# Small parameter loads of a hybrid encoder layer: other queue, other place in the lead-in

## Chip, cores and metric

The kernel runs on one core of a Trainium2 chip. Such a core has a matmul engine (TensorE, PE in the profile; PEld is its loading of weights), VectorE (DVE), ScalarE (ACT), GpSimd (POOL) and SyncE (SP), which here only issues transfers. 16 DMA engines carry the transfers. The metric is the device time in microseconds (us) of one execution, and the median over several runs.

## What is computed

One step of a streaming encoder layer, for 512 prompt rows and 64 sample rows of width 1024 that share the parameters. Cut to what matters here:

```
mod = silu(c) @ w_ada + b_ada                     # 6 vectors of 1024 for each of the two groups
sh1, sc1, gt1, sh2, sc2, gt2 = split(mod, 6)
h = rms_normalize(x) * g_norm_mix * (1 + sc1) + sh1
q, k, v, qi, ki, wi, z, xbc, dt, gate_logits = split(h @ w_in)
...  # sparse attention: an indexer (qi, ki, wi) picks 256 keys for each query
xbc_c = silu(causal_conv(xbc, w_conv, b_conv))    # and a Mamba-2 scan over it
y = rms_normalize(y * silu(z)) * g_ssm_norm
x = x + gt1 * ((g_attn * (o @ w_branch_attn) + g_ssm * (y @ w_branch_ssm)) @ w_out)
h2 = rms_normalize(x) * g_norm_ffn * (1 + sc2) + sh2
x = x + gt2 * ((silu(gate) * up) @ w_down)        # gate, up = split(h2 @ w_gate_up)
```

The conditioning vectors c are two rows of 1024 (4 KB each). b_ada has 6144 numbers (24 KB), g_norm_mix and g_norm_ffn 1024 each (4 KB), g_ssm_norm 2048 (8 KB), b_conv 4096 (16 KB).

## The kernel before

All work is first recorded as a list of operations with their dependences by a planner, the class `Plan`. Its method `order` gives every operation an estimated duration and a place on its engine: at each step it takes the operation that can start first, by due times and priorities. The method `emit` then issues the operations, all by the same line, so every instruction of the trace carries L569, and the names of its tiles tell what it is. `R.after([...])` adds a dependence for the planner alone. On the chip each engine works its list off in order, and waits by semaphores for what an instruction reads, and for a buffer that it writes over to be free.

Products are made of high and low parts: a weight piece `raw` is loaded, ScalarE rounds it to `wh`, VectorE makes the rest `wl`, and three matmuls (`wh` with the high and the low part of h, `hTh` and `hTl`, and `wl` with `hTh`) sum into `mm`. PE's results stand in eight banks: `mm` (two tiles of two banks), and `px` and `py` with two each, which the operations take in turn. A tile `px` that is asked for anew is one of two banks, and the first writer waits for the last reader of what stood there.

The lead-in: SyncE loads the conditioning rows (`rowsS`), the five blocks of x (`xt`, four of 512 KB and one of 256 KB), then blocks of w_ada (`adr`) and w_in (`raw`). GpSimd issues loads by a software queue (q0), SyncE by the common hardware queue (q1). Vectors arrive as rows of 128 and are turned by a PE transpose (a matmul with the unit matrix `ident`), so that each number stands in its own partition: `rowsS` (16 rows, for `cu`, `cth` and `sil`, the silu of c), `rowsD` (48 rows, b_ada, for `badc`) and `rowsA` (64 rows: both norm gains, the scan's gain and the convolution's bias, for `vc`). For each x block ScalarE squares and sums the rows (`xn` written, a scratch result), VectorE scales them to `xn`, and PE transposes x and `xn`. The matmuls `py<-adr,sil` give the shift and scale of the first norm, from which h is made; some later w_ada columns are summed by VectorE (`aacc`).

After the indexer's projections come the scan's step sizes: PE sums decay exponents with a triangular matrix into a `px` bank (`px<-e,tri`, called `pacs` in the code) and into a `py` bank, VectorE negates the first (`nacs`) and adds the second (`wst`). PE then goes on with the projection that gives k and v, `mm<-wh,hTh` with 256 columns, and `py<-kis,qis`, the indexer's scores.

The list `ropes` holds the operations that end the rotary step of the indexer's query heads.

Of the kernel before, what the change touches and what calls it, by code (L numbers as in the profile page):

```python
# [5 lines left out]
F32 = mybir.dt.float32  # L6
# [3 lines left out]
OP = mybir.AluOpType  # L10
# [3 lines left out]
P = 128  # L14
# [562 lines left out]
def build(tc, I, O):  # L577
    R = Plan(tc)
    vec, act, pool, pe, sync = R.vec, R.act, R.pool, R.pe, R.sync
    cp = R.mkpool("const")  # L580
# [5 lines left out]
    sp = R.mkpool("start")  # L586
# [4 lines left out]
    def px(name, tag="px"):  # L591
        return psum.tile([P, 512], F32, name=name, tag=tag, bufs=2)
# [5 lines left out]
    ident = cp.tile([P, P], F32, name="ident")  # L598
# [60 lines left out]
    def pair_order(r):  # L659
        return ORD0 if r == 0 else (1, 7, 6, 2, 5, 4, 3)  # L660
# [162 lines left out]
            pe.transpose(out, ident, ident)  # L823

    rowsS = sp.tile([16, P], F32, name="rowsS")
    for r0, src in ((0, I["c_prompt"][0]), (8, I["c_sample"][0])):
        sync.dma_start(rowsS[r0:r0 + 8], src.rearrange("(a b) -> a b", b=P))
    xt = []
    for tb in range(5):
        n = P if tb < 4 else NS  # L830
        t = sp.tile([P, D], F32, name=f"xt{tb}")
        src = x_p[tb * P:(tb + 1) * P] if tb < 4 else x_s
        sync.dma_start(t[:n], src)
        xt.append(t)


    sil = adp.tile([P, 8, 32], F32, name="sil")
# [7 lines left out]
    pc = px("pc", "py")  # L845
# [90 lines left out]
    def rstd_of(ss, out, n, rows, denom):  # L936
        vec.tensor_scalar(out, ss, 1.0 / denom, EPS, op0=OP.mult, op1=OP.add)
        pow_mhalf(out, out, n)
# [13 lines left out]
    rs = sp.tile([P, 5], F32, name="rs")  # L952
    pool.memset(rs, 1.0)
    turned, xn_ops = [], []
    rowsD = sp.tile([48, P], F32, name="rowsD")
    pool.dma_start(rowsD, I["b_ada"][0].rearrange("(a b) -> a b", b=P))
    rowsA = sp.tile([64, P], F32, name="rowsA")
    for r0, n, src in ((0, 8, I["g_norm_mix"][0]), (8, 8, I["g_norm_ffn"][0]), (16, 16, I["g_ssm_norm"][0]), (32, 32, I["b_conv"][0])):
        pool.dma_start(rowsA[r0:r0 + n], src.rearrange("(a b) -> a b", b=P))
    for tb in range(5):  # L960
        n = P if tb < 4 else NS
        xn = sp.tile([P, D], F32, name=f"xn{tb}", tag="xn", bufs=4)
        act.activation(xn[:n], xt[tb][:n], AF.Square, accum_out=rs[:n, tb:tb + 1])
        rstd_of(rs[:n, tb:tb + 1], rs[:n, tb:tb + 1], 1, n, D)
        xn_ops.append(vec.tensor_scalar(xn[:n], xt[tb][:n], rs[:n, tb:tb + 1], None, op0=OP.mult))
        for k4 in range(2):
            p = px(f"pxn{tb}_{k4}")
            for j in range(4):
                kt = 4 * k4 + j
                turned.append(pe.transpose(p[:, j * P:j * P + n], xn[:n, kt * P:(kt + 1) * P], ident[:n, :n]))  # L970
            act.activation(xnT[:, 4 * k4:4 * k4 + 4, tb * P:tb * P + n], p.rearrange("p (k q) -> p k q", k=4)[:, :, :n], AF.Copy)
        if tb == 2:
            badc = cp.tile([P, 48], F32, name="badc")
            with R.after([turned[-1]]):
                pe.transpose(pc[:, 64:112], rowsD, ident[:48, :48])
            vec.tensor_copy(badc, pc[:, 64:112])
            vc = cp.tile([P, 64], F32, name="vc")
            with R.after([turned[-1]]):
                pe.transpose(pc[:, 128:192], rowsA, ident[:64, :64])
            vec.tensor_copy(vc, pc[:, 128:192])  # L980
            g_mix, g_ffn = vc[:, 0:8], vc[:, 8:16]
    rowsB = sp.tile([P, P], F32, name="rowsB")
    rowsC = sp.tile([96, P], F32, name="rowsC")
    gsh = cp.tile([P, 16], F32, name="gsh")
    vec.tensor_scalar(gsh, vc[:, 16:32], 0.5, None, op0=OP.mult)
    wc = cp.tile([P, 4, 32], F32, name="wc")
    bc_ = cp.tile([P, 32], F32, name="bconv")
    stc = cp.tile([P, 3, 32], F32, name="stc")
    vec.tensor_scalar(bc_, vc[:, 32:64], 0.5, None, op0=OP.mult)

    A1 = cp.tile([P, 8, 2], F32, name="A1")
    hTh = hp.tile([P, 8, T], F32R, name="hTh")
# [30 lines left out]
    with R.prio(-1500):  # L1023
        for tb in range(5):
            n = P if tb < 4 else NS
# [23 lines left out]
    t = px("pwc")  # L1049
# [196 lines left out]
    ropes, masked = [], []  # L1246
# [75 lines left out]
    acs_d = R.dram([32, T], F32, name="acs_d")  # L1322
    sync.dma_start(acs_d, acsT)

    with R.after([ropes[1]]):
        for dst, src in xst:
            sync.dma_start(dst, src)
# [4 lines left out]
    for b in range(5):  # L1332
        n = P * (b + 1) if b < 4 else T
# [3 lines left out]
    for b in (4, 1, 2, 3):  # L1337
        smp = b == 4
        n = T if smp else P * (b + 1)
# [109 lines left out]
    for kv in range(NKV):  # L1449
# [21 lines left out]
        for un in units + [None]:  # L1471
            nxt = None
            if un is not None:
                b, qs, k0, n, nk, v0, w = un
# [316 lines left out]
    for a in range(8):  # L1791
# [5 lines left out]
        with R.prio(MPRIO):  # L1797
            vec.scalar_tensor_tensor(t2(g), t2(g), 1.0, ps, op0=OP.add, op1=OP.mult)
            vec.tensor_tensor(m, m, g, OP.add)
            for c0, n, d0, dn in ((0, NP_, 0, HP), (NP_, NS, HP, HS)):  # L1800
                src = t2(m[:, c0:c0 + n])
# [23 lines left out]
    with R.prio(PTP):  # L1825
        for c0 in PT:
            w = I["w_out"][0]
            b = pair_raw[c0] = {"qs": [PAIRW[p] for p in pair_order(c0 // 256)]}
# [54 lines left out]
    for r in range(NPW):  # L1883
# [3 lines left out]
        t, u, v, zz = ha[:, 0], ha[:, 1], hb[:, 0], hb[:, 1]  # L1887
# [39 lines left out]
    for hf in range(2):  # L1927
# [17 lines left out]
        for j in range(4):  # L1945
            t = y2[j, hf][:, :, 0:TH]
# [185 lines left out]
    for i, (f, w, x, b, starts, *p) in enumerate(steps):  # L2132
# [6 lines left out]
        if i < N0:  # L2139
            if not starts:  # L2140
                with R.prio(4000):
                    n = TH if b[1] == "1" else TW
# [357 lines left out]
```

## Time and profile before

| | |
|---|---|
| median of three runs (lowest, highest) | 1350.63 us (1348.82, 1352.64) |
| the profiled execution | 1350.98 us, of which the span 1349.3 us |
| granted clock of PE over the span | 0.998 of 2.4 GHz |
| moved by DMA | 202.88 MB, mean 150 GB/s |
| software queue (q0) | 5152 packets, 14.87 MB |

The span reaches from the first to the last instruction that the profile shows; the execution's own time is 1.7 us longer. The median is over unprofiled runs. All rows further down come from the one profiled execution.

### The profile page before, as it was taken

How to read it: one execution, taken by the hardware profiler on the slowest of the kernel's cores; microseconds unless marked ns; L12 is line 12 of the kernel's file. 1: busy time of each engine (PE TensorE's matmuls, PEld its weight loads, DVE VectorE, ACT ScalarE, POOL GpSimd, SP SyncE). 2: the span in 40 equal slices, each digit the busy share in tenths (PEclk: the TensorE clock that was granted, in tenths of full speed). 3: DMA queues.
4: the chain of work that ended last, by engine and by line, in shares of the span. 5: the costliest groups of instructions: out<-in, count | busy, mean ns of one | idle time of the engine just before them, and what ended most of it. 6: DMA issues, size and time to landing. Idle time of an engine off the chain costs nothing.

```text
span 1349.3 us, 27924 instructions
## 1 busy us (share of the span) xinstructions
PE 1334.7 (99%) x10601; PEld 1299.7 (96%) x10601; DVE 1162.0 (86%) x2373; ACT 775.9 (58%) x1641; POOL 250.4 (19%) x386
## 2 busy tenths in 40 slices
PE   7999999999999999999999999999999999999998
PEld 6999999999999999999999999999999999999998
DVE  5687999887778798888887798898799999988997
ACT  4564333777776766666565442227576666665553
POOL 2322011330300235545463300000000000000000
PEclk9999999999999999999999999999999999999999
DMA  9874435664854464454445797665433344424352
GB/s 286 249 195 117 112 109 150 153 171 99 196 126 119 132 175 116 115 149 131 131 122 165 231 306 245 208 196 176 117 95 97 99 130 131 124 83 137 100 159 63
DMA packets 269975, 202.88 MB, mean 150 GB/s; under 512 B 26048, under 2 KB 240176, under 8 KB 269840
## 3 DMA queue, kind: packets, MB, share of 16 engines
q1 hardware_dynamic: 264400, 186.09, 47.1%
q0 software_dynamic: 5152, 14.87, 5.7%
q8 instruction: 83, 1.36, 0.4%
q14 instruction: 52, 0.43, 0.1%
q10 hardware_dynamic: 288, 0.13, 0.0%
HBM read 158.33 MB, written 28.96 MB: 139 GB/s over the span
## 4 chain that ended last, share of the span: by engine, by line
PE 91%; DVE 4%; DMA 2%; issue 1%; ACT 1%; SPq 1%; DVEq 0%; ACTq 0%
PE mm L569 63%; PE py L569 16%; PE px L569 12%; DMA adr<-in_w_ada 1%; DMA raw<-in_w_in 1%; DMA xt<-in_x_prompt 1%; DVE aacc L569 1%; DVE wl L569 1%; SPq L569 1%; DVE g L569 0%; ACT wh L569 0%; DVE wh L569 0%; DVE y L569 0%; DVE tok L569 0%; DVE x L569 0%
## 5 line engine op out<-in xcount | busy, mean ns | idle before, releaser
L569 PE MATMUL mm<-hTl,wh 128*128 128x288 f32 (+1 forms) x1088 | 246.9, 302 | 1.1 <-DVE hTl L569 1.1
L569 PE MATMUL mm<-hTh,wh 128*128 128x288 f32 (+1 forms) x1088 | 244.9, 302 | 0.6 <-ACT wh L569 0.5
L569 PE MATMUL mm<-hTh,wl 128*128 128x288 f32 (+1 forms) x1088 | 244.3, 302 | 0.0
L569 ACT ACTIVATE wh<-raw 128x1024 fp32r<-128x1024 f32 (+3 forms) x143 | 137.9, 966 | 124.7 <-PE mm L569 106.7
L569 PEld LDWEIGHTS mm<-hTl,wh 128*128 128x128 f32 (+1 forms) x1088 | 177.1, 189 | 4.0 <-DVE hTl L569 1.8
L569 PEld LDWEIGHTS mm<-hTh,wh 128*128 128x128 f32 (+1 forms) x1088 | 176.0, 189 | 3.9 <-ACT hTh L569 0.8
L569 PEld LDWEIGHTS mm<-hTh,wl 128*128 128x128 f32 (+1 forms) x1088 | 176.1, 189 | 2.2 <-issue 0.7
L569 DVE TENSOR_TENSOR wl<-raw,wh 128x1024 fp32r<-128x1024 f32 (+2 forms) x94 | 117.3, 1250 | 18.2 <-ACT wh L569 16.9
L569 POOL DMA_DIRECT2D wl<-raw x24 | 20.9, 872 | 463.7 <-PE px L569 314.0
L569 PE MATMUL mm<-oh,wh 128*128 128x288 f32 (+1 forms) x424 | 94.8, 299 | 0.3 <-ACT sum L569 0.3
L569 DVE SCALAR_TENSOR_TENSOR cu<-xc,wc,cu 128x579 f32<-128x579 f32 x96 | 83.9, 875 | 2.0 <-ACT cu L569 1.0
L569 PE MATMUL mm<-oh,wl 128*128 128x288 f32 (+1 forms) x360 | 79.9, 298 | 0.0
L569 PE MATMUL mm<-ol,wh 128*128 128x288 f32 (+1 forms) x276 | 72.4, 298 | 0.0
L569 PEld LDWEIGHTS mm<-oh,wh 128*128 128x128 f32 x424 | 70.4, 188 | 1.1 <-ACT sum L569 0.5
L569 DVE SCALAR_TENSOR_TENSOR aacc<-adr,sil,aacc 128x512 f32<-128x512 f32 x84 | 62.8, 785 | 7.0 <-DMA adr<-in_w_ada 7.0
L569 PEld LDWEIGHTS mm<-oh,wl 128*128 128x128 f32 x360 | 59.7, 188 | 0.3 <-issue 0.2
L569 PE MATMUL mm<-yl,wh 128*128 128x288 f32 x256 | 55.0, 295 | 0.0
L569 PE MATMUL mm<-yh,wh 128*128 128x288 f32 x256 | 54.9, 295 | 0.0
L569 PE MATMUL mm<-wl,hTh 128*128 128x256 f32 x192 | 54.6, 285 | 0.3 <-DVE wl L569 0.3
L569 PE MATMUL mm<-wh,hTl 128*128 128x256 f32 x192 | 54.7, 286 | 0.0
L569 PE MATMUL mm<-yh,wl 128*128 128x288 f32 x256 | 54.4, 294 | 0.0
L569 PE MATMUL mm<-wh,hTh 128*128 128x256 f32 x192 | 53.6, 283 | 0.0
(584 smaller groups left out, 3940.9 us busy)
## 6 DMA issues: line engine op xcount, KB each, us to landing
raw<-in_w_in SPq DMA_DIRECT2D x80, 512.0 KB, 4.2
adr<-in_w_ada SPq DMA_DIRECT2D x36, 512.0 KB, 5.4
raw<-in_w_gate_up SPq DMA_DIRECT2D x22, 512.0 KB, 3.9
wl<-raw POOLq DMA_DIRECT2D x21, 512.0 KB, 4.6
rawu<-in_w_gate_up SPq DMA_DIRECT2D x20, 512.0 KB, 4.0
bc<-acs_d SPq DMA_DIRECT2D x32, 256.0 KB, 3.5
raw<-in_w_branch_ssm SPq DMA_DIRECT2D x16, 512.0 KB, 5.0
gate_d<-sg SPq DMA_DIRECT2D x16, 288.0 KB, 2.2
```

The lines of the kernel that those rows point to most:

```text
L569: getattr(engines[x.eng], x.fn)(*[real(a) for a in x.args], **{k: real(v) for k, v in x.kw.items()})
```

## The change

The two conditioning rows are loaded by SyncE behind the second x block rather than ahead of the first. `rowsD` takes g_norm_mix with it: 56 rows, two loads by SyncE behind the x blocks where GpSimd's software queue had loaded them, one transpose and one copy. `rowsA` keeps the other three vectors (56 rows); its three loads are issued by SyncE after the indexer's queries, its transpose goes to a new `px` tile near the scan's step sizes, and `gffn` becomes a tile of its own. GpSimd issues five loads fewer, SyncE five more. The planner makes its order anew from this list.

```diff
     rowsS = sp.tile([16, P], F32, name="rowsS")
-    for r0, src in ((0, I["c_prompt"][0]), (8, I["c_sample"][0])):
-        sync.dma_start(rowsS[r0:r0 + 8], src.rearrange("(a b) -> a b", b=P))
     xt = []
     for tb in range(5):
...
         sync.dma_start(t[:n], src)
         xt.append(t)
+        if tb == 1:
+            for r0, src in ((0, I["c_prompt"][0]), (8, I["c_sample"][0])):
+                sync.dma_start(rowsS[r0:r0 + 8], src.rearrange("(a b) -> a b", b=P))
...
-    rowsD = sp.tile([48, P], F32, name="rowsD")
-    pool.dma_start(rowsD, I["b_ada"][0].rearrange("(a b) -> a b", b=P))
-    rowsA = sp.tile([64, P], F32, name="rowsA")
-    for r0, n, src in ((0, 8, I["g_norm_mix"][0]), (8, 8, I["g_norm_ffn"][0]), (16, 16, I["g_ssm_norm"][0]), (32, 32, I["b_conv"][0])):
-        pool.dma_start(rowsA[r0:r0 + n], src.rearrange("(a b) -> a b", b=P))
+    rowsD = sp.tile([56, P], F32, name="rowsD")
+    for r0, n, src in ((0, 48, I["b_ada"][0]), (48, 8, I["g_norm_mix"][0])):
+        sync.dma_start(rowsD[r0:r0 + n], src.rearrange("(a b) -> a b", b=P))
...
         if tb == 2:
-            badc = cp.tile([P, 48], F32, name="badc")
+            badc = cp.tile([P, 56], F32, name="badc")
             with R.after([turned[-1]]):
-                pe.transpose(pc[:, 64:112], rowsD, ident[:48, :48])
-            vec.tensor_copy(badc, pc[:, 64:112])
-            vc = cp.tile([P, 64], F32, name="vc")
-            with R.after([turned[-1]]):
-                pe.transpose(pc[:, 128:192], rowsA, ident[:64, :64])
-            vec.tensor_copy(vc, pc[:, 128:192])
-            g_mix, g_ffn = vc[:, 0:8], vc[:, 8:16]
+                pe.transpose(pc[:, 64:120], rowsD, ident[:56, :56])
+            vec.tensor_copy(badc, pc[:, 64:120])
+            g_mix = badc[:, 48:56]
     rowsB = sp.tile([P, P], F32, name="rowsB")
     rowsC = sp.tile([96, P], F32, name="rowsC")
+    rowsA = cp.tile([56, P], F32, name="rowsA")
+    g_ffn = cp.tile([P, 8], F32, name="gffn")
     gsh = cp.tile([P, 16], F32, name="gsh")
-    vec.tensor_scalar(gsh, vc[:, 16:32], 0.5, None, op0=OP.mult)
...
-    vec.tensor_scalar(bc_, vc[:, 32:64], 0.5, None, op0=OP.mult)
...
+    with R.after([ropes[3]]):
+        for r0, n, src in ((0, 32, I["b_conv"][0]), (32, 16, I["g_ssm_norm"][0]), (48, 8, I["g_norm_ffn"][0])):
+            sync.dma_start(rowsA[r0:r0 + n], src.rearrange("(a b) -> a b", b=P))
+    t = px("pwd")
+    pe.transpose(t[:, 0:56], rowsA, ident[:56, :56])
+    vec.tensor_scalar(bc_, t[:, 0:32], 0.5, None, op0=OP.mult)
+    vec.tensor_scalar(gsh, t[:, 32:48], 0.5, None, op0=OP.mult)
+    vec.tensor_copy(g_ffn, t[:, 48:56])
```

How the order of the engines changes is shown at two places. The first is the head of SyncE's list, before:

```order
L569 DMA rowsS_140<-in_c_prompt 8x128
L569 DMA rowsS_140<-in_c_sample 8x128
L569 DMA xt_0_141<-in_x_prompt 128x1024
L569 DMA xt_0_142<-in_x_prompt 128x1024
L569 DMA xt_0_143<-in_x_prompt 128x1024
L569 DMA xt_0_144<-in_x_prompt 128x1024
L569 DMA xt_0_145<-in_x_sample 64x1024
L569 DMA adr_158<-in_w_ada 128x4x256
```

and of the change:

```order
L569 DMA xt_0_142<-in_x_prompt 128x1024
L569 DMA xt_0_143<-in_x_prompt 128x1024
L569 DMA rowsS_141<-in_c_prompt 8x128
L569 DMA rowsS_141<-in_c_sample 8x128
L569 DMA xt_0_144<-in_x_prompt 128x1024
L569 DMA xt_0_145<-in_x_prompt 128x1024
L569 DMA xt_0_146<-in_x_sample 64x1024
L569 DMA rowsD_151<-in_b_ada 48x128
L569 DMA rowsD_151<-in_g_norm_mix 8x128
L569 DMA adr_158<-in_w_ada 128x4x256
```

Two x blocks now stand first, and the two `rowsD` loads stand between the x blocks and w_ada. (The number behind a name is the tile's buffer, counted anew in each kernel.)

The second place is PE's list where the projection of k begins, behind the sums with the triangular matrix, before:

```order
L569 MATMUL px_112<-e_0_704,tri_72 128x32
L569 MATMUL py_110<-e_0_704,ones_71 128x32
L569 MATMUL mm_115<-wh_103,hsS_128 128x256
L569 MATMUL mm_115<-wl_106,hsS_128 128x256
L569 MATMUL mm_114<-wh_101,hTh_126 128x256
L569 MATMUL mm_114<-wl_104,hTh_126 128x256
L569 MATMUL mm_114<-wh_101,hTl_127 128x256
L569 MATMUL mm_114<-wh_101,hTh_126 128x256
L569 MATMUL mm_114<-wl_104,hTh_126 128x256
```

and of the change:

```order
L569 MATMUL px_113<-e_0_697,tri_72 128x32
L569 MATMUL py_111<-e_0_697,ones_71 128x32
L569 MATMUL mm_116<-wh_104,hsS_129 128x256
L569 MATMUL mm_116<-wl_107,hsS_129 128x256
L569 MATMUL mm_115<-wh_102,hTh_127 128x256
L569 MATMUL mm_115<-wl_105,hTh_127 128x256
L569 MATMUL mm_115<-wh_102,hTl_128 128x256
L569 MATMUL mm_115<-wh_102,hTh_127 128x256
L569 MATMUL px_113<-ident_70,rowsA_76 128x56
L569 MATMUL mm_115<-wl_105,hTh_127 128x256
```

The transpose of `rowsA` stands between the fourth and the fifth matmul of the projection, and it writes `px_113`, the buffer that the sums `px<-e,tri` were written to four matmuls of the projection earlier. VectorE's list at this place, of the change:

```order
L569 SCALAR_TENSOR_TENSOR aacc_0_711<-adr_713,sil_120,aacc_0_711 128x512
L569 SCALAR_TENSOR_TENSOR aacc_0_712<-adr_713,sil_120,aacc_0_712 128x512
L569 TENSOR_TENSOR acsT_696<-tmpb_674,acsT_696 128x576
L569 TENSOR_TENSOR wl_106<-raw_100,wh_103 128x1024
L569 TENSOR_SCALAR nacs_90<-px_113 128x160
L569 TENSOR_TENSOR wst_91<-py_111,nacs_90 128x160
```

In before the same six operations stand here in the same order. The reader of the sums, `nacs`, comes behind the split of a weight piece (`wl`).

Up to about 85 us the engines' lists are otherwise alike, from there to about 700 us they differ by small exchanges, and from about 700 us to the end they are the same.

## Rows read from the trace of the kernel before

**Rows 1.** The page's table of engines: busy time, share of the span, instructions.

```profile
PE 1334.7 (99%) x10601; PEld 1299.7 (96%) x10601; DVE 1162.0 (86%) x2373; ACT 775.9 (58%) x1641; POOL 250.4 (19%) x386
```

**Rows 2.** Stretches: length, busy (x) of PE, PEld, DVE, ACT, POOL, clock, DMA share, GB/s.

```profile
0.00:25.00 25.00, 18.97 (x178) 15.34 (x178) 13.84 (x36) 15.23 (x28) 7.65 (x25) 1.00 0.92 264
25.00:45.00 20.00, 18.75 (x260) 15.19 (x261) 10.51 (x23) 6.86 (x13) 2.85 (x5) 0.91 1.09 332
...
102.00:700.00 598.00, 597.66 (x4739) 579.98 (x4738) 509.08 (x1110) 370.32 (x818) 181.29 (x275) 1.00 0.52 134
```

**Rows 3.** Chain of waits, 0 to 60 us: start, length, what.

```profile
2.94 8.98 DMA xt<-in_x_prompt
```

**Rows 4.** SyncE's issues, 0 to 10 us: start, length of the issue, transfer.

```profile
0.81 0.39 SPq L569 DMA_DIRECT2D rowsS<-in_c_prompt  x1
...
1.59 1.79 SPq L569 DMA_DIRECT2D xt<-in_x_prompt  x4
```

**Rows 5.** SyncE's issues, 35.6 to 36.4 us.

```profile
35.61 0.81 SPq L569 DMA_DIRECT2D adr<-in_w_ada  x1
```

**Rows 6.** DMA issues of that stretch: count, size, us from issue to landing.

```profile
adr<-in_w_ada SPq DMA_DIRECT2D x1, 512.0 KB, 7.9
```

**Rows 7.** PE's timeline, 40 to 44.5 us: start, length, operation.

```profile
43.76 0.97 PE L569 MATMUL py<-adr,sil 128*32 128x128 f32 x28
```

**Rows 8.** Stretches of the lead-in, columns as in rows 2.

```profile
7.00:9.00 2.00, 1.33 (x11) 1.10 (x11) 1.62 (x5) 1.05 (x3) 0.58 (x1) 1.00 1.00 371
9.00:12.00 3.00, 2.61 (x21) 2.16 (x21) 2.92 (x7) 2.18 (x5) 1.11 (x2) 1.00 1.08 184
```

**Rows 9.** DMA queues, 7 to 9 us: packets, MB, share of 16 engines.

```profile
q0 software_dynamic: 103, 0.02, 5.6%
```

**Rows 10.** PE's timeline, 99 to 102 us; in brackets idle time before, and its releaser.

```profile
99.33 0.28 PE L569 MATMUL mm<-wl,hTh 128*128 128x256 f32 x1
...
100.27 0.28 PE L569 MATMUL mm<-wh,hTh 128*128 128x256 f32 x1
100.82 0.38 PE L569 MATMUL mm<-wl,hTh 128*128 128x256 f32 x1 [0.27 <-DVE wl L569]
101.49 0.53 PE L569 MATMUL py<-kis,qis 128*128 128x288 f32 x2 [0.28 <-DVE wst L569]
101.86 0.28 PE L569 MATMUL mm<-wh,hTl 128*128 128x256 f32 x1
```

**Rows 11.** VectorE's timeline, 97 to 102 us.

```profile
100.69 0.32 DVE L569 TENSOR_SCALAR nacs<-px 128x160 f32<-128x160 f32 x1
101.11 0.33 DVE L569 TENSOR_TENSOR wst<-py,nacs 128x160 f32<-128x160 f32 x1
```

**Rows 12.** PE's timeline, 107.7 to 109 us, around another transpose.

```profile
108.00 0.28 PE L569 MATMUL mm<-wl,hTh 128*128 128x256 f32 x1
108.25 0.33 PE L569 MATMUL py<-ident,ra 128*128 128x128 f32 x1
...
108.54 0.28 PE L569 MATMUL mm<-wh,hTh 128*128 128x256 f32 x1
```

**Rows 13.** SyncE's issues, 92 to 101 us.

```profile
92.92 1.90 SPq L569 DMA_DIRECT2D adr<-in_w_ada  x1
...
98.99 0.35 SPq L569 DMA_DIRECT2D adr<-in_w_ada  x1
```

**Rows 14.** DMA issues: small loads, 0 to 60 us and at 113 us.

```profile
rowsB<-in_w_conv SPq DMA_DIRECT2D x1, 64.0 KB, 5.9
...
acs_d<-acsT SPq DMA_DIRECT2D x1, 72.0 KB, 1.8
```

**Rows 15.** ScalarE's timeline, 0 to 7 us.

```profile
0.81 1.28 ACT L569 ACT_TABLE_LOAD   x1 [0.81 <-PEq L2488]
...
5.88 1.04 ACT L569 ACTIVATE xn<-xt 128x1024 f32<-128x1024 f32 x1
```

**Rows 16.** One stretch of the lead-in, columns as in rows 2.

```profile
26.00:29.00 3.00, 3.00 (x38) 2.25 (x37) 1.92 (x2) 0.00 (x0) 0.00 (x0) 0.50 1.09 354
```

## Prediction

> **What bounds the kernel now.** The engine table comes first: TensorE (PE) is busy 99% of the span, VectorE 86%, ScalarE 58%, GpSimd 19% [rows 1]. An edit therefore counts only where PE stands still, or where it adds work to PE. The stretches say where that is: of the first 25 us PE is busy 18.97, so 6 us are idle; of the next 20 it is busy 18.75, at a mean granted clock of 0.91; of the 598 us from 102 to 700 it is idle for 0.34 [rows 2]. The change touches the first 45 us and a place near 100 us, where PE is full except for two short waits.
>
> What the lead-in waits for is read from the chain of waits: the transfer of an x block, from 2.94 us and 8.98 long [rows 3], with PE's first work behind it. So the lead-in is one stream of loads, and PE, VectorE and ScalarE work on what lands. SyncE's issues give its start: the conditioning rows from 0.81, the x blocks from 1.59 [rows 4]. From 25 to 45 us the stream runs at 332 GB/s [rows 2]. Its end is the last 512 KB of w_ada that PE needs before the projections run freely: issued at 35.61 [rows 5], 7.9 us to landing [rows 6], so 43.5; PE takes up that group of 28 small matmuls at 43.76 [rows 7]. What brings this landing forward is gained once, and what puts it back is lost once; behind it PE is full.
>
> **The change part by part.** The sum is made against the profiled execution's own 1350.98 us. The median of three runs is 1350.63, so 0.35 comes off at the end.
>
> *The start of the stream.* The conditioning rows leave SyncE's head. The first x load is then issued where the first of them was, at 0.81 instead of 1.59: 0.78 us earlier [rows 4]. From there to 43.5 transfers follow each other, so I let the whole lead-in move by it: -0.78. Bounds: all of it, and nothing (rival C). The rows themselves are 8 KB in both kernels, and who needs them (the w_ada matmuls) waits for larger loads anyway.
>
> *Less in the stream.* The three parameter vectors that move to about 95 us are 28 KB; at 332 GB/s [rows 2] they leave 28.7/332 = 0.09 us: -0.09. The 28 KB that stay (biases and the first gain) pass through SyncE now; two issues of 0.39 [rows 4] stand behind x loads of which several are under way, and only later issues feel them. 0, with an upper bound of 0.8 that rival C covers.
>
> *Five loads off the software queue.* GpSimd has four fifths of its time free [rows 1], so its issue time is worth nothing. Beside that there is only what these loads do to the others. From 9 to 12 us the transfers run at 184 GB/s with a share of 1.08, while from 7 to 9 they ran at 371 [rows 8]. In those fast 2 us 103 packets of the software queue were moved as well [rows 9]. Since the stream ran at full rate beside them, I put the effect at 0; the other bound is rival A. The Trainium skill, page DMA: Bandwidth & Descriptors, section Issuing engines are not separate DMA queues, says that loads of any engine run on the same 16 DMA engines and interleave, and that spreading them saves issue time alone; by it this step gives 0, which the 7 to 9 us bear out.
>
> *The transpose at PE's k projection.* The three moved loads and the transposing matmul now stand near 100 us. In the order the matmul comes after four matmuls of the k projection, where before one stood that ran at 99.33 [rows 10]. It writes the buffer that held the running sums (px), and VectorE reads these for `nacs` at 100.69, for 0.32 [rows 11]. VectorE's row of work before it is the same in both orders, ending with the split of a weight piece, so the buffer comes free at 100.69+0.32 = 101.01. PE stops at 99.33 and goes on at about 101.06; the 0.05 for the signal are what lies between the end of VectorE's `wst`, 101.11+0.33 = 101.44 [rows 11], and PE's matmul that waits for it, 101.49 [rows 10]. What does the stop cost in the end? The transpose itself adds what the same kind of transpose adds elsewhere: with `ra` the matmul before it starts at 108.00 and the second one behind it at 108.54 [rows 12]; two intervals of 0.118 belong to the matmuls (eight of them lie between 99.33 and 100.27 [rows 10]), so 0.54-0.24 = 0.30. Then nine matmuls that before ran in the time of the stop, 9 x 0.118 = 1.06; then the pair `kis,qis` with 0.37 (101.49 to 101.86) and the matmul of `wl` with 0.12. Before, PE waited for that `wl` (0.27) and for `wst` (0.28) [rows 10]; both are long done now, so these 0.55 are swallowed. The matmul that started at 101.86 starts at 101.06+0.30+1.06+0.37+0.12 = 102.91: **+1.05**. Bounds: +0.30 if PE comes there so late that the buffer is free (rival B), and more if the data are not there. For that: SyncE has issued the w_ada piece of 92.92 after 1.90 us, and issues the next at 98.99 [rows 13]; three issues of 0.39 fit between and end at 96.0. The load then has 5.0 us until 101.01. A small load with little beside it lands after 1.8 us, one in the crowded lead-in after 5.9 [rows 14], so at worst 0.9 comes on top; I take 0, since the queue is nearer to the first. Behind PE's stop the projection's readers (ScalarE's and VectorE's work on k and v) come later by the same 1.05, and have time.
>
> *VectorE's three small operations* (two scalings, one copy) replace three of the same kind at the start; 86% busy, and their readers (convolution, norms) stand far behind: 0. *ScalarE's table load* of 1.28 us now stands behind the wait for the first x block, since the square of that block is its first work; before it ran at 0.81 during idle time, and the square at 5.88 [rows 15]. The square needs the block, so that had landed by 5.88; with the stream 0.78 earlier it lands by 5.10, and the square begins by 5.10+1.28 = 6.38, at worst 0.5 late. ScalarE has idle time there (15.23 busy of 25 [rows 2]) and its `cth`, which stood ahead of the first square, goes behind the second; the x block of [rows 3] is waited for much later. So 0.
>
> **Sum:** -0.78 - 0.09 + 1.05 = +0.18, that is 1351.16 for an execution like the profiled one, and 1351.16 - 0.35 = **1350.8** for the median.
>
> **The rivals.**
> A, faster: the software queue makes the slow stretch of 9 to 12 us, and without it the stream keeps its rate. Lost there: 3 x (332-184)/332 = 1.34 us; then 1350.8 - 1.34 = 1349.5. For it: the slow stretch follows at once on the software queue's packets, and these are what the change takes out of it. Against it: the 7 to 9 us, where they ran at full rate. In a sentence beside it: the Trainium skill, page DMA: Bandwidth & Descriptors, section Latency and other measured facts, reports two of the 16 DMA engines slower than the rest and guesses at the software queue's descriptor rings as the cause, and no row here shows single engines. Chance 0.18.
>
> B, faster: PE arrives at the transpose when the buffer is free, because VectorE gains more in the lead-in than PE or PE is held earlier by a weight piece. Only the 0.30 stay: 1350.8 - 0.75 = 1350.0. Chance 0.12.
>
> C, slower: the first load pays a start that the small rows paid before (ring fetch, first access), and the two added issues hold the w_ada loads, so the 0.78 isn't gained: 1350.8 + 0.78 = 1351.6. Chance 0.12.
>
> D, slower: PE's clock. From 26 to 29 us the granted clock is 0.50, half, that is 1.2 GHz of 2.4, behind a lead-in in which PE was idle for a quarter of the time [rows 2, 16]; the price of that stretch is 20 x (1-0.91) = 1.8. The stop of 1.7 us near 100 us could bring such a stretch again: 1350.8 + 1.8 = 1352.6. Against it: the first 25 us, a quarter of them idle, were themselves granted 1.00 [rows 2], and ahead of this stop PE is full. It decides from the point where the stop grows, above all if the loads are late. The Trainium skill, page TensorE: Matmul & The Clock Gate, Part 1, says that activity releases the clock and idleness takes it back; by it a longer stop is what to fear, and D is that. Chance 0.10.
>
> E, slower beyond doubt: the orders of 85 to 700 us differ piece by piece (durations and due times have moved). There PE has 0.34 us of idle time to win and much to lose; with VectorE at 509 of 598 us [rows 2] a conversion that comes 0.3 us late at each of some 15 weight pieces gives 4 us or more: 1355. Chance 0.08.
>
> The rest, 0.40, is the forecast.
>
> **How the numbers follow.** The likeliest is 1350.8, its own range 1349.9 to 1351.7. A reaches 1349.5, D 1352.6; A with B, with the half-clocked stretch of the lead-in shorter too, 1347.7; part of E 1353.6. So 1347.7 to 1353.6 leaves out most of E and a little below. 0.3% is 4.05 us (the three runs of before lie 3.8 apart): faster is under 1346.6, which needs A, B and the 1.8 of the clock at once: 0.09. Slower is over 1354.7: E and D with late loads, 0.11. Same 0.80.
>
> **What would show it.** Start: first x load at 0.8, and PE full from 43.0 instead of 43.8. Place near 100 us: a wait of PE of about 1.7 us before the matmul on `rowsA`, released by VectorE's `nacs`; released by a DMA, the loads were late. A: over 300 GB/s from 9 to 12 us. D: a stretch at 0.50 just after 101. E: PE idle from 102 to 700 over 0.34 us. I am wrong above all if PE's stop is not there or if the new order's small waits add up.

## The result

The changed kernel takes 1359.08 us in the median of six runs (1356.79 to 1361.78), the kernel before 1350.21 in its six (1348.82 to 1352.64). The ratio is 1.0068 with an interval of 1.0058 to 1.0079: 0.7% slower, 8.9 us, where 0.2 us were forecast and 1353.6 was the end of the range.

### The profile page after: what moved, and what is told of

It reads as the page before. It is cut to its first block, busy times and chain, and to the rows that moved or that the text cites. A ratio compares the mean times of both kernels' runs of the same rounds, so it can differ in the third digit from the quotient of the medians.

```text
span 1355.1 us, 27934 instructions
## 1 busy us (share of the span) xinstructions
PE 1336.5 (99%) x10601; PEld 1299.3 (96%) x10601; DVE 1165.7 (86%) x2373; ACT 775.4 (57%) x1641; POOL 255.6 (19%) x381
## 4 chain that ended last, share of the span: by engine, by line
PE 85%; DVE 5%; ACT 4%; DMA 3%; issue 2%; POOL 0%; SPq 0%; ACTq 0%; POOLq 0%; DVEq 0%
PE mm L569 59%; PE py L569 15%; PE px L569 11%; DVE cu L569 1%; ACT wh L569 1%; DMA bc<-acs_d 1%; DMA xt<-in_x_sample 1%; DMA raw<-in_w_in 1%; DVE wl L569 1%; ACT dec L569 1%; DMA adr<-in_w_ada 0%; ACT xc L569 0%; ACT wl L569 0%; ACT qst L569 0%; SPq L569 0%
## 5 line engine op out<-in xcount | busy, mean ns | idle before, releaser
L569 DVE SCALAR_TENSOR_TENSOR cu<-xc,wc,cu 128x579 f32<-128x579 f32 x96 | 86.9, 905 | 2.5 <-ACT cu L569 1.7
L569 ACT ACTIVATE P<-lg,mn 128x128 f32<-128x128 f32 (+4 forms) x72 | 41.6, 579 | 23.8 <-DVE mn L569 23.1
L569 ACT ACTIVATE dec<-dec,nacs 128x128 f32<-128x128 f32 x128 | 42.3, 393 | 22.2 <-POOL dec L569 18.6
```

Source lines behind the costliest of these rows:

```text
L569: getattr(engines[x.eng], x.fn)(*[real(a) for a in x.args], **{k: real(v) for k, v in x.kw.items()})
```

## The profile after

The profiled execution took 1356.79 us, the fastest of the six, so it shows some 6 of the 8.9 us. The page's table of engines, to be held against [rows 1]:

```profile
PE 1336.5 (99%) x10601; PEld 1299.3 (96%) x10601; DVE 1165.7 (86%) x2373; ACT 775.4 (57%) x1641; POOL 255.6 (19%) x381
```

The same instructions but for five of GpSimd's, nearly the same busy time; so PE has waited. The stretches of [rows 2], with the same columns, say where:

```profile
0.00:25.00 25.00, 18.44 (x175) 15.12 (x175) 12.94 (x33) 14.79 (x28) 4.33 (x19) 1.00 0.95 263
25.00:45.00 20.00, 18.86 (x263) 15.44 (x264) 10.74 (x23) 7.33 (x14) 4.01 (x5) 0.91 1.10 350
...
102.00:700.00 598.00, 595.03 (x4704) 574.56 (x4703) 508.51 (x1105) 365.26 (x806) 185.06 (x272) 1.00 0.50 134
```

PE's busy time in the lead-in is nearly as before. From 102 to 700 us PE is idle for 2.97 us instead of 0.34. Two instructions that both programs have date the loss: the matmul `mm<-wh,hTl` behind the first pair `kis,qis` starts at 101.86 in before [rows 10] and, below, at 101.90 after; the last `py<-ident,zl` of the program starts at 1343.98 in before and at 1350.83 after. So this execution is even with before at 102 us, and 6.8 us behind at the end.

The start, in SyncE's issues of the changed kernel (start, length, transfer):

```profile
0.81 0.88 SPq L569 DMA_DIRECT2D xt<-in_x_prompt  x2
1.74 0.38 SPq L569 DMA_DIRECT2D rowsS<-in_c_prompt  x1
...
4.64 0.34 SPq L569 DMA_DIRECT2D rowsD<-in_g_norm_mix  x1
6.22 3.03 SPq L569 DMA_DIRECT2D adr<-in_w_ada  x4
```

The first x load is issued at 0.81, as forecast. But the w_ada loads, issued from 4.05 in before (SyncE's timeline of before, the row that follows those of [rows 4]), now wait until 6.22. SyncE's own waits from 0 to 14 us say for what (who waited for whom: us in total, times, longest):

```profile
SPq L569 <- DMA xt<-in_x_prompt: 4.6, 3, 2.2
```

SyncE stands until x blocks have landed, three times and 4.6 us in all; in before this view has no such row. The stretches of [rows 8] after the change:

```profile
7.00:9.00 2.00, 1.73 (x12) 1.29 (x13) 1.67 (x6) 1.15 (x4) 0.58 (x1) 1.00 1.10 342
9.00:12.00 3.00, 2.18 (x19) 1.94 (x20) 2.58 (x6) 2.58 (x6) 0.56 (x1) 1.00 1.04 176
```

The slow stretch from 9 to 12 us is there as before, 176 GB/s against 184, with no load of the software queue left in the lead-in: rival A is out. What the last group of w_ada matmuls of the lead-in says, PE's timeline at the place of [rows 7]:

```profile
43.65 1.08 PE L569 MATMUL py<-adr,sil 128*32 128x128 f32 x32
```

That is 0.11 us sooner than in before (the group has 32 matmuls in both kernels; the window of [rows 7] ends inside it). PE does not wait for a load there, in before either: its only wait from 36 to 45 us of before is

```profile
PE mm L569 <- DVE hTl L569: 0.2, 1, 0.2
```

Near 100 us the forecast stop is there. PE's timeline (in brackets the idle time and its releaser), then VectorE's:

```profile
98.69 0.28 PE L569 MATMUL mm<-wh,hTh 128*128 128x256 f32 x1
100.15 0.26 PE L569 MATMUL px<-ident,rowsA 56*128 56x56 f32 x1 [1.19 <-DVE nacs L569]
100.35 0.39 PE L569 MATMUL mm<-wl,hTh 128*128 128x256 f32 x1
...
101.78 0.29 PE L569 MATMUL mm<-wl,hTh 128*128 128x256 f32 x1
101.90 0.28 PE L569 MATMUL mm<-wh,hTl 128*128 128x256 f32 x1
```

```profile
96.64 1.42 DVE L569 SCALAR_TENSOR_TENSOR aacc<-adr,sil,aacc 128x512 f32<-128x512 f32 x2 [1.68 <-DMA adr<-in_w_ada]
...
99.78 0.32 DVE L569 TENSOR_SCALAR nacs<-px 128x160 f32<-128x160 f32 x1
```

PE waits for `nacs` before it may write the bank, and VectorE is at `nacs` when a w_ada piece has let its list go on (1.68 us of waiting for `adr`). From the fourth matmul of the projection to `mm<-wh,hTl` it is 101.90 - 98.69 = 3.21 us; in before, from the matmul ahead of the one at 99.33, it is 101.86 - 99.20 = 2.66 (PE's rows are 0.12 to 0.13 apart there, [rows 10]). This execution lost 0.55 there, and had come to the fourth matmul 0.51 sooner (98.69 against 99.20).

The rest lies behind. The scan stage of the layer (445 to 740 us) in before and after, columns as in [rows 2]:

```profile
445.00:740.00 295.00, 294.93 (x2499) 284.83 (x2497) 252.54 (x462) 188.31 (x456) 136.31 (x244) 1.00 0.50 139
```

```profile
445.00:740.00 295.00, 291.30 (x2457) 279.35 (x2456) 253.41 (x454) 185.64 (x450) 144.17 (x243) 1.00 0.48 135
```

PE starts 42 matmuls fewer in this stretch, by estimate some 5 us at the 0.12 of [rows 10] each; 3.7 us of it are idle time, and the rest stands in no row. PE's waits from 445 to 740 us in the changed kernel, where the same view of before has no row:

```profile
PE py L569 <- DVE xw L569: 1.6, 1, 1.6
PE py L569 <- DVE xb L569: 0.9, 1, 0.9
PE py L569 <- ACT bt L569: 0.6, 2, 0.4
PE py L569 <- ACT dec L569: 0.2, 1, 0.2
```

The longest single wait, as the chain of waits of the changed kernel tells it (start, length, what), and PE's timeline there:

```profile
727.82 5.02 DMA bc<-acs_d
...
732.90 0.64 POOL decS L569
...
733.83 0.33 ACT decS L569
734.16 0.95 ACT wh L569
735.11 0.64 ACT xc L569 x3
...
736.22 0.27 ACT bt L569
...
736.52 0.44 DVE xw L569
...
737.00 0.70 PE py L569 x2
```

```profile
737.00 0.70 PE L569 MATMUL py<-xw,bt 128*128 128x256 f32 x2 [1.59 <-DVE xw L569]
```

A load of the scan's decay rows (`bc`) lands late; GpSimd masks it (`decS`), ScalarE's exponentials of it stand ahead of a weight conversion (`wh`) and of `bt`, and PE waits 1.59 us at the product `py<-xw,bt`.

## Experiments

Two theories at the start. Theory 1: the edits are nearly free where they stand, but they made the planner choose another order behind 112 us, and that order is worse. Theory 2: the moved loads and the late transpose cost the time themselves.

To tell them apart, an order can be pinned. At the end of the kernel file the planner's result is replaced by a list of all operations in a given sequence:

```diff
+def replay(self):
...
+    self.order()
+    d = np.frombuffer(zlib.decompress(base64.b85decode(ORDER)), np.int16)
+    seq = [int(i) for i in np.cumsum(d.astype(np.int64))]
...
+    for k in [None] + seq:
...
+Plan.run = replay
```

The operations and their data stay as they are; `ORDER` holds the sequence, with the moved operations behind the neighbour that they have in the changed kernel.

All times are in us; the ratio is to runs of before on the same chip, with its 95% interval. (The chips differ from group to group; the median of before there lies between 1349.85 and 1350.48.)

| kernel | loads of | sequence from 112 us | median | ratio (interval) |
|---|---|---|---|---|
| e1 | after | each engine's list of before | 1355.15 | 1.0040 (1.0027 to 1.0054) |
| e2 | before | each engine's list of after | 1363.17 | 1.0098 (1.0083 to 1.0113) |
| e3 | after | after, 228 to 445 lists of before | 1359.88 | 1.0069 (1.0056 to 1.0081) |
| e4 | after | after, from 445 lists of before | 1356.88 | 1.0050 (1.0037 to 1.0062) |
| f1 | after | before | 1352.62 | 1.0020 (1.0011 to 1.0029) |
| f2 | before | after | 1357.47 | 1.0063 (1.0051 to 1.0075) |
| f3 | after | after, 228 to 445 before | 1359.53 | 1.0071 (1.0059 to 1.0083) |
| f4 | after | after, from 445 before | 1352.94 | 1.0021 (1.0010 to 1.0033) |
| g1 | after | after, three loads exchanged | 1358.28 | 1.0056 (1.0043 to 1.0069) |
| g2 | before | before, three loads exchanged | 1364.75 | 1.0108 (1.0095 to 1.0121) |
| g3 | after | before, transpose 16 matmuls later | 1349.98 | 0.9999 (0.9990 to 1.0007) |
| g4 | before and late part | before | 1351.86 | 1.0013 (1.0003 to 1.0023) |
| h1 | after | after, PE's list of before in the scan | 1400.70 | 1.0376 (1.0356 to 1.0396) |
| h2 | after | after, lists of ScalarE, VectorE, GpSimd of before in the scan | 1391.33 | 1.0309 (1.0295 to 1.0323) |
| h3 | after | after, GpSimd's list of before in the scan | 1370.79 | 1.0148 (1.0134 to 1.0162) |
| h4 | before | before, PE's list of after in the scan | 1383.11 | 1.0236 (1.0216 to 1.0255) |
| k1 | after | planner's own, transpose in the other bank | 1350.70 | 1.0005 (0.9996 to 1.0013) |
| k2 | before and late part | planner's own | 1358.60 | 1.0063 (1.0049 to 1.0076) |

**The first four (e1 to e4)** pinned what each engine does one after the other, but wrote the program out across the engines in a sequence of my own.

e1, expected: 

> The changed kernel with all its moved loads and its late transpose, but from 112 us on every engine works off its list in the order of the kernel before. Theory 1 (the planner's new order behind 112 us makes the loss): about 1350, within 2 us of before, and PE's waits ahead of py<-xw,bt near 503, 629, 659 and 737 us gone. Theory 2 (the moved loads and transpose themselves make it): 1357 to 1362 as the changed kernel.

e2, expected: 

> The kernel before with all its loads where they were, but from 112 us on in the order of the changed kernel. Theory 1: 1357 to 1361, with waits of PE ahead of py<-xw,bt between 480 and 740 us. Theory 2: 1349 to 1352.

e3, expected: 

> The changed kernel with the order of before from 228 to 445 us alone (attention stage). Theory 1: the slip of 1.2 us that PE has gathered there goes, the rest stays: 1356 to 1359. If the loss of the later stage is a consequence of the slip in this one: 1351 or less. Theory 2: as the changed kernel, 1357 to 1362.

e4, expected: 

> The changed kernel with the order of before from 445 us on (scan stage). Theory 1: the slip of 5 to 6 us of that stage goes: 1351 to 1354. Theory 2: as the changed kernel, 1357 to 1362.

Neither theory fits all four: e1 and e4 lie between the kernels, e2 above both, and e3 is as the changed kernel. The fault was in the experiment. Where two engines only read the same PSUM tile, here VectorE's `xdt<-px` and ScalarE's `bt<-px`, the program makes the one that is written out second wait for the first (so I read its waits; there is nothing else that ties the two). In e1 `xdt` waits for ScalarE in 29 of 32 places, in before in 23; in e2 in 6, in the changed kernel in 19. So these four measure their own sequence too, and were done again with the full sequence.

**The same with the full sequence (f1 to f4).**

f1, expected: 

> As e1 (all moved loads and the late transpose, order of before from 112 us on), but the program is also written out across the engines in the sequence of before. In e1 each engine had the order of before, and still VectorE's xdt<-px waited for ScalarE's bt<-px in 29 of 32 places where it does so in 23 before: the two read one PSUM tile, and who is written out first makes the other wait. Theory 1 (the planner's new sequence behind 112 us makes the loss): 1349 to 1352, PE without waits over 0.5 us ahead of py<-xw,bt. Theory 2 (the loads and the transpose themselves): 1355 to 1362, as e1 and the changed kernel.

f2, expected: 

> As e2 (loads of before, order of the changed kernel from 112 us on), in the changed kernel's full sequence across the engines. Theory 1: 1357 to 1361, with PE's waits ahead of py<-xw,bt at 503 and 737 us of 0.9 and 1.6. Theory 2: 1349 to 1352.

f3, expected: 

> The changed kernel with the full sequence of before between 228 and 445 us (attention stage). Theory 1: its share of the slip, about 1.2 us by the two traces, goes: 1356 to 1358.5. If the later waits follow from the earlier slip: 1352 or less. Theory 2: no change, 1359.

f4, expected: 

> The changed kernel with the full sequence of before from 445 us on (scan stage). Theory 1: 5 to 6 us go: 1351 to 1354, and PE's waits ahead of py<-xw,bt of 0.4 to 1.6 us are gone. Theory 2: no change, 1359.

Against e1 and e2 the times fall by 2.5 and 5.7 us, with every engine's own list unchanged: so much hangs on who is written out first. And now theory 1 holds for most of the loss. With the loads of before and the new sequence (f2) the time is 1357.5, 7.6 us above before. With all edits and the sequence of before in the scan stage alone (f4) it is 1352.9, 6.1 below the changed kernel; in the attention stage alone (f3) it changes nothing that these runs can show. The scan stage of f4 and of f2, columns as in [rows 2]:

```profile
445.00:740.00 295.00, 294.92 (x2500) 285.00 (x2499) 253.07 (x463) 189.24 (x456) 134.52 (x243) 1.00 0.49 137
```

```profile
445.00:740.00 295.00, 290.55 (x2449) 278.29 (x2449) 252.37 (x453) 184.96 (x449) 143.43 (x243) 1.00 0.48 135
```

PE is full in the one and idle for 4.5 us in the other, with the moved loads in the first and without them in the second. But f1 missed its window upwards by a little: 2.7 us over before remain with the edits alone. Its trace shows them near 100 us, PE's timeline and the stretch behind it:

```profile
97.80 0.28 PE L569 MATMUL mm<-wh,hTh 128*128 128x256 f32 x1
100.20 0.35 PE L569 MATMUL px<-ident,rowsA 56*128 56x56 f32 x1 [2.13 <-DVE nacs L569]
100.48 0.58 PE L569 MATMUL mm<-wl,hTh 128*128 128x256 f32 x1
100.86 0.41 PE L569 MATMUL mm<-wh,hTl 128*128 128x256 f32 x1
101.08 0.41 PE L569 MATMUL mm<-wh,hTh 128*128 128x256 f32 x1
...
103.26 0.41 PE L569 MATMUL mm<-wh,hTl 128*128 128x256 f32 x1
```

```profile
100.00:104.00 4.00, 3.80 (x17) 3.70 (x18) 3.45 (x7) 1.05 (x3) 0.60 (x2) 0.50 0.84 220
```

The stop is 2.13 us long in this execution, and behind it the granted clock is 0.50: the matmuls start 0.21 apart instead of 0.12. From the fourth matmul of the projection (97.80) to `mm<-wh,hTl` it is 5.46 us against 2.66 in before: 2.80. The matmuls stay 0.21 apart until 106.25, by estimate 1.3 us more. This is more than f1 loses in the median: the profiled execution is the slowest of its eleven (1354.11), and PE came to the place 1.40 us sooner than in before. That the place makes f1's loss is for g3 to show.

**Three loads, and the late transpose (g1 to g4).** In g1 and g2 three rows change places in SyncE's list, of this kind (the first of the three, as the changed kernel has it, and g1):

```diff
-L569 DMA raw_101<-in_w_in 128x8x128
 L569 DMA bc_5025<-acs_d 128x4x64
+L569 DMA raw_101<-in_w_in 128x8x128
```

g3 has the list of f1 with one matmul moved. g4 is the kernel before with

```diff
+    rowsL = cp.tile([56, P], F32, name="rowsL")
+    g_ffn = cp.tile([P, 8], F32, name="gffn")
...
+    with R.after([ropes[3]]):
+        for r0, n, src in ((0, 32, I["b_conv"][0]), (32, 16, I["g_ssm_norm"][0]), (48, 8, I["g_norm_ffn"][0])):
+            sync.dma_start(rowsL[r0:r0 + n], src.rearrange("(a b) -> a b", b=P))
+    t = px("pwd")
+    pe.transpose(t[:, 0:56], rowsL, ident[:56, :56])
```

and the three VectorE operations from it.

g1, expected: 

> The changed kernel with three exchanges in SyncE's list alone: the scan's decay rows of the sample chunk (bc, 32 KB read out to 128 partitions) are issued ahead of the weight piece (raw, 512 KB) that stood ahead of them, in the groups 3, 5 and 7, as in the order of before. Theory 1a (these three loads, late behind a weight piece, hold GpSimd's decS, then ScalarE's list, then PE): GpSimd's waits for bc of 3.9, 4.3 and 5.5 us (at 582, 657, 733) fall to about 2, PE's waits at 629, 660 and 737 us shrink, and the time falls by 2 to 4 us, to 1355 to 1357. Theory 1b (the loss of the scan stage is the order of the computing engines, as in VectorE's longer operations beside GpSimd): no change, 1358 to 1360.

g2, expected: 

> The reverse on the kernel before: the same three decay rows are issued behind the weight piece. Theory 1a: 1352 to 1354, with GpSimd's waits for bc of 4 us and more and a wait of PE ahead of py<-xw,bt behind each. Theory 1b: 1349.5 to 1351.

g3, expected: 

> As f1 (all moved loads, sequence of before from 112 us on), but the transpose of rowsA stands 16 matmuls later in PE's list, behind the pair kis,qis, where VectorE has read the sums long before. Theory A (f1's 2.7 us are PE's stop for nacs, and the half clock that follows it): no wait of over 0.3 us ahead of that matmul, clock 1.00 from 100 to 112, 1349.5 to 1351 (a little under before if the earlier start of the stream counts). Theory B (the 2.7 come of the lead-in or of the later loads): 1352 to 1353.5.

g4, expected: 

> The kernel before in its own sequence, with its loads, to which the late part alone is added: three loads near 94 us, the transpose after four matmuls of the k projection, and bconv, gsh and gffn from it (the early transposed vectors then serve the first norm alone). Theory A: PE's stop for nacs of 1.0 to 2.1 us is there, 1351.5 to 1353 as f1. Theory B: 1349.5 to 1351.

My reading of the long wait at 737 us, that the decay rows come late because a weight piece stands ahead of them, fell: in g1 the time is not clearly other than that of the changed kernel (1355.47 to 1361.08 against 1356.79 to 1361.78), and GpSimd's timeline still has the wait:

```profile
734.52 0.41 POOL L569 TENSOR_SCALAR_AFFINE_SELECT decS<-bc 64x256 f32<-64x256 f32 x1 [4.77 <-DMA bc<-acs_d]
```

The same exchange costs the kernel before 14.9 us, far more than either theory said (g2, PE's timeline; the two other places have waits of 3.48 and 2.72):

```profile
662.36 1.04 PE L569 MATMUL py<-xw,bt 128*128 128x256 f32 x2 [3.59 <-DVE xw L569]
```

So a late decay row can hold PE, but in the changed kernel the issue order of these three is not what makes it late. (PE's wait at `py<-xw,bt` near 737 us is 0.68 in g1 instead of 1.59, without a clear gain in the time.) SyncE's waits show what stands ahead of the row, in the changed kernel from 718.5 to 727.2 us, then in g1 from 720.8 to 729.4:

```profile
SPq L569 <- POOL cvo L569: 7.8, 1, 7.8
```

```profile
SPq L569 <- POOL cvo L569: 7.8, 1, 7.8
```

In both SyncE stands for GpSimd at an earlier `bc` load, and the decay row goes out behind that one. In before SyncE stands nearly as long for GpSimd (7.5 us), but only until 720.06. No run takes this wait away by itself.

g3 settles the 2.7: with the transpose 16 matmuls later all moved loads together cost nothing, 0.9999 (by its interval between 1.4 us less and 0.9 us more). PE's only wait there is that for `wst`, which before has too [rows 10]. g4 agrees: the late part alone, in the sequence of before, has the stop (1.96 us in its trace, and 0.57 of the clock from 100 to 104 us). Its runs spread from 1348.89 to 1355.68, those of g3 from 1348.65 to 1352.17.

**Which engine's order (h1 to h4).** One engine's list, or three, are taken from the other kernel in the scan stage; `ORDER` alone differs.

h1, expected: 

> The changed kernel; from 445 to 745 us (scan stage) PE alone works in the order of before, the other engines keep the new order. Theory P (PE's new order asks for products, py<-xw,bt above all, before VectorE and ScalarE have made what they read): most of the stage's 6 us go, 1352.5 to 1355. Theory C (the new order of ScalarE, VectorE and GpSimd makes them late, whatever PE does): 1357.5 to 1360, as the changed kernel.

h2, expected: 

> The reverse part: in the same stretch ScalarE, VectorE and GpSimd work in the order of before, PE and SyncE keep the new one. Theory P: 1357.5 to 1360. Theory C: 1352.5 to 1354.5, and PE's waits ahead of py<-xw,bt go.

h3, expected: 

> Only GpSimd's list is that of before in this stretch. If GpSimd's order alone makes it (its decS waits for a load with other work behind it): 1353 to 1355.5. Theory P and a theory C that rests on ScalarE's or VectorE's order: 1357.5 to 1360.

h4, expected: 

> The kernel before, with PE alone in the new order in this stretch. Theory P: 1353 to 1357, with PE's waits ahead of py<-xw,bt. Theory C: 1349.5 to 1351.5. If the loss needs both (PE's order fits neither), h1 and h4 both lose: over 1355 each.

All four missed the windows of theories P and C: every mixture costs 20 to 50 us. Only the last branch of h4 came true, that h1 and h4 both lose, and the loss is far larger than any of them said. The sequence across the engines is that of neither plan here, and e1 and e2 have shown that this too has a price (2.5 and 5.7 us). The lists fit one another, and an order of one engine with the others' orders of another plan is here worse than both plans. No engine's list carries the 6 us alone in a way that this could show, and which decision in the new sequence costs them stays open.

**Which edit turns the planner (k1, k2).** k1 is the changed kernel and one line:

```diff
+    px("skip")
     t = px("pwd")
```

k2 is g4 without the pinned sequence.

k1, expected: 

> The changed kernel with one line more: a px tile that nobody uses is asked for ahead of pwd, so that the transpose of rowsA takes the other px bank, that of the transposed sums, which ScalarE has read. Nothing is pinned; the planner makes its own order: the transpose then stands some 90 rows later in PE's list, and the scan stage comes out in the order of before but for 6 places. Theory 1 (the late transpose in the bank of the sums makes both losses: PE's stop at 100 us, and the turn of the planner to the scan order that costs 6 us): 1349 to 1351.5, no stop ahead of rowsA, 112 to 740 us as before. If the moved loads cost by themselves: 1353 or more.

k2, expected: 

> The kernel before with the late part alone, as g4, but with the planner's own order, in which the scan stage comes out as in the changed kernel but for 5 places. Theory 1: the whole loss, 1357 to 1361, against 1351.9 for the same loads in the sequence of before (g4). If the other two parts of the change bear some of the loss: 1354 to 1356.

Both came out as theory 1 said. k2, without the two other parts of the change, has the whole loss, 1358.60. k1, with all of the change but for the bank of one transpose, has none, 1350.70. (The unused tile also puts every later `px` tile back into the bank that it has in before. f1, f4 and g3 have these banks as the changed kernel has them, and their scan stage is full, so on the chip this alone costs nothing. Whether it turns the planner no timed run shows apart; the planner alone, without the chip, gives the same lists when a second unused tile behind `pwd` turns the later banks round again.) The scan stage of k2, then of k1:

```profile
445.00:740.00 295.00, 290.07 (x2448) 278.02 (x2447) 251.94 (x452) 184.95 (x448) 143.32 (x243) 1.00 0.48 134
```

```profile
445.00:740.00 295.00, 294.91 (x2502) 284.94 (x2502) 251.40 (x462) 188.26 (x456) 138.00 (x245) 1.00 0.50 139
```

And PE's timeline of k1 near 100 us, which is again that of [rows 10], with the two short waits of before:

```profile
100.25 0.28 PE L569 MATMUL mm<-wh,hTh 128*128 128x256 f32 x1
100.93 0.38 PE L569 MATMUL mm<-wl,hTh 128*128 128x256 f32 x1 [0.40 <-DVE wl L569]
101.59 0.53 PE L569 MATMUL py<-kis,qis 128*128 128x288 f32 x2 [0.28 <-DVE wst L569]
```

No version beat the kernel before: the best, g3 and k1, are even with it.

## Why the prediction was wrong

The step that failed is the one that stood in the sum with no term: that the planner's new order from 85 to 700 us costs nothing. It appeared as rival E, with a chance of 0.08, 4 us and VectorE's late conversions as its cause. It was the main case: 6.1 us by f4, in the scan stage alone (7.6 by f2, which has all of the new sequence), and by waits for `xw`, `xb` and `bt` rather than for weight pieces. E's 0.3 us and 15 pieces stood in no row. That PE is full in a stretch says how well the old sequence fits, and nothing of another sequence; "PE has 0.34 us to win and much to lose" was the right sentence, and its chance was far too low.

*The start of the stream, -0.78.* The first load is issued at 0.81 as said, but the gain is not there (rival C). Two things were wrong. Loads do not simply follow each other from the first one on: with the new head of its list SyncE stands until x blocks have landed, in each of the 13 traces that have it (3.1 to 4.6 us) and in none of the seven with the old one, and the first w_in load goes out at 10.12 to 11.81 instead of 8.04 to 9.24. And the w_ada group at 43.76 was not the landing that the lead-in ends with: PE comes to it from other work without a wait, so an earlier landing there gives nothing. The group starts 0.11 us earlier in this execution; over all traces it is at 42.56 to 45.19 with the new start and at 41.70 to 45.17 with the old one, so no gain shows, rather a loss that the spread hides. All moved loads together are 0.9999 in g3.

*Five loads off the software queue, 0:* right. The slow stretch of 9 to 12 us stayed. The Trainium skill, page DMA: Bandwidth & Descriptors, section Issuing engines are not separate DMA queues, has loads of all engines share the 16 DMA engines, with nothing but issue time to gain from the choice; g3 and k1 agree.

*The transpose, +1.05:* the mechanism is as forecast, released by `nacs`, with the loads long landed (issued from 93.82, landed after 2.7 to 3.0 us; the 1.8 us of [rows 14] that the bound used belong to a store); the size of the stop is not fixed. It was 1.19 us (0.55 lost) in the profiled execution and 0.6 to 2.1 in the others with this transpose. PE's arrival varies with the lead-in, `nacs` comes after a load: the fourth matmul and `nacs` start at 97.80 and 99.83 in f1, at 100.38 and 101.11 in f4, so the sooner PE comes, the longer it stands. With the clock it is 2.6 us by f1 against g3.

*The clock, rival D at 0.10:* it happens often. Of 13 traces that have this stop, the clock from 100 to 104 us is below 1.00 in seven: 0.50 after 2.13 us of standing, 0.57 after 1.96 and 1.78, 0.70 after 1.74, 0.59 after 1.63, and 0.61 and 0.76 after 1.22 and 0.87. It stayed at 1.00 after 1.38, 1.19 and four shorter ones, and in the seven traces without this stop. D's price of 1.8 was near: in f1 the 25 matmuls from 100.86 to 106.25 took by estimate 2.4 us longer than at the full clock. That the lead-in is granted 1.00 with more idle time was no argument against it. The Trainium skill, page TensorE: Matmul & The Clock Gate, Part 1, says that idleness brings the throttle back; these rows agree as far as it fell at this place only where PE had stood.

*VectorE's and ScalarE's small edits, 0:* right. The table load now runs from 4.62 us, and the first square starts at 5.92 instead of 5.88 [rows 15]:

```profile
4.62 1.28 ACT L569 ACT_TABLE_LOAD   x1 [4.62 <-DMA xt<-in_x_prompt]
5.92 1.06 ACT L569 ACTIVATE xn<-xt 128x1024 f32<-128x1024 f32 x1
```

So the account is: moved loads 0 within about 1 us, the stop and the clock behind it about 2.6, the new sequence of the scan stage about 6.1, together 8.7 of the 8.9 us (with f2's 7.6 it would be 10.2, so the fit is no closer than 1.5 us). Both come from one edit, the transpose that takes the bank of the sums; which decision in the new sequence costs its 6 us stays open.

## What to carry to other kernels

Where a planner makes the order anew, a small edit has two prices: its own, and that of the order that the planner turns to; the second can be several times the first, far behind the edit. Pin the old order under the new edit, and the new order under the old code, and the two are told apart; pin the sequence across the engines too. A tile that asks for a buffer takes over the wait for its last reader, so the bank of a late, unimportant operation is worth choosing.

## What the runs showed of the hardware that was not expected

PE's clock fell to half behind stops of 0.9 to 2.1 us in a place ahead of which PE had been full (in f1 52.51 of the 55 us from 45 to 100, the stop taking most of the rest). In f1 the matmuls stayed 0.21 us apart until 106.25, 6 us after PE went on. Stops of 1.1 to 1.4 us left it at 1.00 in four traces, and stops of 0.87 and 1.22 did not in two others, so the length of the stop alone does not decide.
